# K and Q convolutions in a lane of their own, scaled outputs in the head's key and query tile, the learned tokens' masks in a stream of their own

## The chip, the core and the metric

The kernel runs on one core of a Trainium2 chip. Its engines are PE (TensorE, matrix products; PEld is its weight load), DVE (VectorE), ACT (ScalarE), POOL (GpSimd) and SP (SyncE, which here issues every DMA). Each engine works through its own list of instructions in a fixed order and stops at an instruction until what that instruction needs is there. The metric is the time of one execution on the device, in microseconds, as the median of several runs.

## What is computed

One layer of a bidirectional encoder: 1024 positions of width 1024, with 16 learned ("meta") tokens in front. The input projection gives queries, keys and values of 8 heads (128 wide), gates and two further branches. The part that the change touches is the gated delta rule, in chunks, forwards and backwards:

```python
qkv = silu(depthwise_conv_centred(concat([q, k, v]), conv_w))      # 5 taps
qc, kc = l2norm(q_heads) * DN_DK ** -0.5, l2norm(k_heads)
beta = sigmoid(b_raw);  g = -exp(A_log) * softplus(a_raw + dt_bias)
# chunk_gated_delta_rule, once forwards and once on the flipped sequence:
g = cumsum(g)
decay = exp(where(tri, g[:, None] - g[None, :], -inf))
lmat = where(strict, beta[:, None] * (k @ k.T) * decay, 0)
sol = triangular_solve(lmat + eye, [v * beta, k * beta * exp(g)])   # u, w
qk = (q @ k.T) * decay
for each chunk:                       # a scan with the state S
    v_new = u - w @ S
    o = (q * exp(g)) @ S + qk @ v_new
    S = S * exp(g_last) + (k * exp(g_last - g)).T @ v_new
o = o_fwd + o_bwd
o = o * rsqrt(mean(o * o) + eps) * norm_w * silu(z)
```

Behind it stand the projection of this output, a short convolution branch, the merge of both by sigmoid gates, an output projection and a SwiGLU feed-forward block. Everything is float32.

## The kernel before

Matrix products of float32 are made of three products of the fast fp32r type: each operand is split into a high part (an ACT cast) and the rest (a DVE subtraction). The delta rule itself uses plain float32 products.

The first half of the program (up to about 985 us) is one long interleaving. Its ground is the **dense** work: column blocks of 128 of the input projection, in the function `dense_steps` (line 332 of the profile), each of 24 products for a stretch of 320 to 512 positions. A block is called a unit: K, Q and V of each head (`u_qkv`), the z gates, the short branch (`u_short`), and as many merge gates as are not left for later. Into it go the **streams** of the delta rule, Python generators of which each runs for one head at a time: `g_decay` (decay masks into the tile PQ: one DMA, DVE additions, ACT exponentials), `g_norm` (transposes of keys and queries to token order; ACT copies the keys and squares both with 17 `Square` instructions, line 545, the token part; then the products k k^T and q k^T, line 583, from which DVE makes the tile NP, line 613), `g_inv` (the triangular inverse: 32x32 blocks by a DVE recurrence, lines 491 and 495, then products at lines 706 to 737 with ACT and DVE copies between them, T at line 708 among them) and `g_scan` (8 steps, forwards and backwards at once, lines 796 to 871, then normalization, scaling, transposes and the store of the output).

The order is found while the program is built. The planner keeps a clock for each engine (`T`), to which every instruction adds an assumed cost. After each three dense products `run_streams` lets every stream step that is due go on, and `pump` gives DVE convolution work while its clock is less than 0.7 us ahead of PE's. That work waits in **lanes**, of which `pump` takes the one with the least weighted time spent; the lane "short" gives way to all others. All convolutions of K, Q and V are in one lane, "conv", first come, first served. One convolution (`conv_job`) is, for each half of the positions, four DVE multiply-adds (line 355), an ACT tanh into a half buffer `rb` (line 360) and a DVE product (line 363). A new row buffer `ra` can be had only when the third job before it is done; if it is not, `force` issues what is left of it at once, whatever the planner's clocks say.

Buffers tie the heads together. The tile `kq` (keys and queries of a head, transposed) has 3 buffers, so K of head h takes that of head h-3 (`u_qkv`, `while freed < h - 2`, where `freed` counts heads whose last scan step has read its keys and queries). NP has 2 buffers: the scan adds up its outputs in the place of products that it has used (`oacc`), and the scaled, transposed and gated output `oT` goes into NP as well, from where it is stored to `o_d`. So NP of head h waits for that store of head h-2:

```python
while done < h - 1 or "PQ" not in st_:
    yield T["pe"] + 100
if h > 1:
    yield heads[h - 2]["stored"]
```

`done` counts finished scans and `stored` is the planner's time of the end plus 4 us. At the end of the scan, for each half: four ACT scalings in place (line 893), four PE transposes, one DVE product into NP (line 899), one store of 256 KB.

The masks of the learned tokens (`Dm`, 16x16 for each head) are made at the end of the stream `g_gates`: a DMA, a wait of 6 us in the planner's time, a DVE addition, eight ACT exponentials. `g_gates` stands in the same list as `g_decay`, so the first head's decay masks come behind it.

Of the kernel before, what the change touches and what calls it, by code (L numbers as in the profile page):

```python
# [16 lines left out]
P = 128  # L17
# [20 lines left out]
def encoder_layer(ctx: ExitStack, tc: tile.TileContext, x, meta, norm1_w, w_in,  # L38
# [208 lines left out]
    lanes = {"conv": [], "short": [], "fs": [], "norm": []}  # L247
    spent = {"conv": 0.0, "short": 0.0, "fs": 0.0, "norm": 0.0}
# [17 lines left out]
    WEIGHT = {"conv": 1.0, "short": 1.0, "fs": 0.33, "norm": 0.1}  # L266
# [34 lines left out]
    def pump():  # L301
        while T["dve"] <= T["pe"] + 700:
            now = max(T["dve"], T["pe"])
            cand = [k for k, q in lanes.items() if q and q[0].ready <= now + 20 + DEP * (k == "fs")]
            if "norm" in cand:
                cand = ["norm"]
            if not cand and any(q and q[0].ready <= now + DEP + 20 for q in lanes.values()):
                T["dve"] = now + DEP
                continue
            if not cand:  # L310
                if not rest or T["dve"] > T["pe"] + 100:
                    return
# [54 lines left out]
    def u_qkv(h, i, w):  # L367
# [163 lines left out]
    def g_norm(h, st_):  # L531
# [34 lines left out]
        nc.vector.tensor_tensor(out=Nm, in0=pt[:META, P:P + META], in1=Dm[:, h], op=ALU.mult)  # L566
# [27 lines left out]
        nc.vector.tensor_scalar(out=Nm, in0=Nm, scalar1=cc[:META, 8, 0:1], scalar2=None, op0=ALU.mult)  # L594
# [150 lines left out]
    def g_scan(h, st_):  # L745
# [142 lines left out]
        yield T["dve"] + 2300  # L888
        for c4 in range(2):
            oT = NP[:, 4 * c4:4 * c4 + 4, 1 - c4]  # L890
            pt = newbank()
            for c in range(4):
                nc.scalar.activation(oacc[4 * c4 + c], oacc[4 * c4 + c], AF.Copy, scale=y[:, 4 * c4 + c:4 * c4 + c + 1])
# [23 lines left out]
    decs, norms, invs, scans = [], [], [], []  # L917
# [28 lines left out]
    def start_streams():  # L946
# [9 lines left out]
        h = ninv  # L956
        if h < H and not invs and heads[h].get("normed"):
# [9 lines left out]
    def run_streams():  # L967
        nonlocal done
        again = True
        while again:  # L970
            again = False
            for q in (scans, invs, norms, decs):
                if q and q[0][1] <= T["pe"]:
                    again = True
                    r = next(q[0][0], None)
                    if r is None:
# [4 lines left out]
                        elif q is not decs:  # L981
# [220 lines left out]
    def g_gates():  # L1202
# [84 lines left out]

        nc.sync.dma_start(Dm, grow[:, 8, 0:1, 0:META].rearrange("h o i -> o h i").broadcast_to([META, 8, META]))
        yield T["pe"] + 6000
        nc.vector.tensor_tensor(out=Dm, in0=Dm, in1=mask2[:META, 0, :META].unsqueeze(1).broadcast_to([META, 8, META]), op=ALU.add)  # L1290
        yield small_v()
        for h in range(H):
            nc.scalar.activation(Dm[:, h], Dm[:, h], AF.Exp, bias=negG2[:META, 8, h:h + 1])
            A(16)
            if h % 2:
                yield T["act"]

    dn = ph1.enter_context(tc.tile_pool(name="dn", bufs=1))
# [632 lines left out]
```

## Time and profile before

| what | value |
|---|---|
| median of 3 runs | 1962.57 us (1962.05 to 1963.68) |
| the profiled execution's own time | 1961.08 us |
| its span, first to last instruction | 1959.4 us |
| granted TensorE clock, mean | 0.999 |
| PE busy | 1941.7 us, 99% of the span |
| DVE busy | 1468.1 us, 75% |
| ACT busy | 867.9 us, 44% |
| POOL busy | 158.4 us, 8% |

Busy times of PE are modelled from the starts of pipelined products, so one product's duration (some 340 ns) overlaps the next one's. In a list of groups the first number behind the bar is the busy time in us, the second the mean of one instruction in ns, the third the idle time of the engine just before these instructions. In a list of waits stand the total in us, how many there were, and the longest. "<-" in front of an engine names what ended a wait. In a timeline the columns are start, duration, engine, line, operation, tiles, shapes and count, and idle time before in brackets.

### The profile page before, as it was taken

Reading aid. Unit: us, or ns where it says so; the run is one execution under the profiler, and the core shown is the slowest. Engines: PE = TensorE matmul, PEld = TensorE weight load, DVE = VectorE, ACT = ScalarE, POOL = GpSimd, SP = SyncE. Lnnn points to the kernel's source line nnn. Section 1 sums busy time; section 2 is a strip of 40 time slices with the busy share of each in tenths; the row PEclk is TensorE's granted clock in tenths of the full one; section 3 lists DMA queues with packets and bytes.
Section 4 is the critical chain, followed back from the end, with each engine's and each line's share of the span. In section 5 each row is a group of like instructions: output and inputs, shape, how many; then the busy total and the mean of one; then the engine's idle time right before and its main releaser. Section 6 shows DMA issues by size and latency. Waiting matters only on the chain.

```text
span 1959.4 us, 31938 instructions
## 1 busy us (share of the span) xinstructions
PE 1941.7 (99%) x11962; PEld 1704.4 (87%) x11962; DVE 1468.1 (75%) x2804; ACT 867.9 (44%) x2014; POOL 158.4 (8%) x457
## 2 busy tenths in 40 slices
PE   8999999999999999999999999999999999999998
PEld 8998899999899999998888888887888888888887
DVE  4778778788887888787358798559787887756574
ACT  5463544646455554533445545234232332324343
POOL 3012112020110202110000000000000000000001
PEclk9999999999999999999999999999999999999999
DMA  4222332323222222224386623332666644587654
GB/s 146 68 76 80 103 99 60 87 60 87 60 76 67 85 65 79 70 69 153 103 310 246 206 88 121 115 119 73 212 232 209 209 165 163 179 279 243 194 181 155
DMA packets 243136, 264.11 MB, mean 135 GB/s; under 512 B 46820, under 2 KB 166933, under 8 KB 240549
## 3 DMA queue, kind: packets, MB, share of 16 engines
q1 hardware_dynamic: 242981, 262.07, 42.1%
q8 instruction: 94, 1.54, 0.3%
q14 instruction: 61, 0.50, 0.1%
HBM read 189.58 MB, written 72.44 MB: 134 GB/s over the span
## 4 chain that ended last, share of the span: by engine, by line
PE 89%; DVE 5%; ACT 3%; issue 1%; DMA 1%; POOL 0%; SPq 0%; POOLq 0%; DVEq 0%; ACTq 0%
PE pm L332 31%; PE pm L1382 5%; PE pd L1382 4%; PE pe L1382 3%; PE pm L1656 3%; PE pm L1658 3%; PE pm L1657 2%; PE pd L1658 2%; PE pd L1656 2%; PE pd L1657 2%; PE pe L1658 2%; PE pe L1656 2%; PE pe L1657 2%; PE pm L1814 1%; PE pm L1815 1%; PE pm L1813 1%
## 5 line engine op out<-in xcount | busy, mean ns | idle before, releaser
L332 PE MATMUL pm<-hTh,wh 128*128 128x512 f32 (+4 forms) x1328 | 483.8, 365 | 0.1
L332 PE MATMUL pm<-hTh,wl 128*128 128x512 f32 (+4 forms) x1328 | 450.5, 340 | 0.0
L332 PE MATMUL pm<-al,wh 128*128 128x512 f32 (+4 forms) x1328 | 449.6, 339 | 0.5 <-DVE al L1047 0.5
L332 PEld LDWEIGHTS pm<-hTh,wl 128*128 128x128 f32 x1328 | 249.1, 188 | 15.5
L332 PEld LDWEIGHTS pm<-hTh,wh 128*128 128x128 f32 x1328 | 250.2, 189 | 13.6 <-ACT hTh L1041 0.2
L332 PEld LDWEIGHTS pm<-al,wh 128*128 128x128 f32 x1328 | 250.4, 189 | 12.9 <-DVE al L1047 0.7
L87 DVE TENSOR_TENSOR al<-raw,ring_h 128x1024 fp32r<-128x1024 f32 x73 | 88.4, 1223 | 63.6 <-ACT ring_h L86 63.2
L86 ACT CAST ring_h<-raw 128x1024 fp32r<-128x1024 f32 x73 | 76.9, 1054 | 109.7 <-PE pd L1815 35.3
L940 DVE TENSOR_TENSOR wl<-raw,wh 128x512 fp32r<-128x512 f32 x122 | 84.1, 690 | 32.0 <-ACT wh L943 27.1
L355 DVE SCALAR_TENSOR_TENSOR kq<-ra,wc,kq 128x520 f32<-128x520 f32 (+1 forms) x128 | 95.9, 749 | 2.3 <-ACT kq L389 1.2
L821 ACT ACTIVATE w<-pd,small 128x128 f32<-128x128 f32 x128 | 40.2, 365 | 124.9 <-PE pd L814 106.4
L128 POOL TENSOR_SCALAR ss<-ss 128x1 f32<-128x1 f32 x13 | 4.6, 353 | 951.1 <-ACT b L1825 603.4
L491 DVE TENSOR_TENSOR tm<-fP,fN 128x135 f32<-128x135 f32 (+23 forms) x248 | 72.1, 291 | 10.0 <-DMA fN<-nd 3.3
L495 DVE TENSOR_TENSOR fP<-fP,tm 128x135 f32<-128x135 f32 (+23 forms) x248 | 71.8, 289 | 7.3
L943 ACT CAST wh<-raw 128x512 fp32r<-128x512 f32 x122 | 74.8, 619 | 0.1
L87 DVE TENSOR_TENSOR raw<-pair,raw 128x1024 fp32r<-128x1024 f32 (+1 forms) x42 | 48.0, 1143 | 30.4 <-ACT raw L86 30.4
L86 ACT CAST raw<-pair 128x1024 fp32r<-128x1024 f32 (+1 forms) x42 | 41.7, 992 | 58.4 <-PE pd L1382 27.5
L87 DVE TENSOR_TENSOR wl<-pair,wh 128x1024 fp32r<-128x1024 f32 (+1 forms) x42 | 48.1, 1144 | 21.7 <-ACT wh L86 21.6
L86 ACT CAST wh<-pair 128x1024 fp32r<-128x1024 f32 (+1 forms) x42 | 41.7, 992 | 46.0 <-PE pd L1382 24.7
L843 DVE SCALAR_TENSOR_TENSOR S<-S,eGl,pd 128x128 f32<-128x128 f32 x104 | 31.8, 344 | 38.2 <-PE pd L831 30.8
L130 POOL TENSOR_TENSOR small<-small,minus_half 128x9 f32<-128x9 f32 x16 | 29.5, 1842 | 353.8 <-DVE small L878 264.0
L661 POOL TENSOR_TENSOR tm<-mP,mN 1x15 f32<-1x15 f32 (+7 forms) x120 | 37.3, 311 | 237.0 <-DMA mN<-ndm 228.7
(660 smaller groups left out, 4945.7 us busy)
## 6 DMA issues: line engine op xcount, KB each, us to landing
raw<-in_w_in_dram SPq DMA_DIRECT2D x64, 512.0 KB
raw<-in_w_gate_up_dram SPq DMA_DIRECT2D x44, 512.0 KB
sums<-in_w_down_dram SPq DMA_DIRECT2D x22, 512.0 KB
t_d<-sums SPq DMA_DIRECT2D x11, 1024.0 KB
raw<-s_d SPq DMA_DIRECT2D x44, 256.0 KB
raw<-t_d SPq DMA_DIRECT2D x44, 256.0 KB
act_d<-b SPq DMA_DIRECT2D x43, 256.0 KB
raw<-act_d SPq DMA_DIRECT2D x33, 256.0 KB
```

What stands on the lines that cost most here:

```text
L86: nc.scalar.copy(hi, src)
L87: nc.vector.tensor_tensor(out=lo, in0=src, in1=hi.bitcast(F32), op=ALU.subtract)
L332: mm(po[:, :n], (wl if j == 2 else wh)[:, k], xl[k][:, t0:t0 + n] if j == 1 else xh[k][:, t0:t0 + n], start=(i == 0), stop=(i == 3 * KT - 1))
L355: nc.vector.scalar_tensor_tensor(out=acc, in0=raw[:, h0 + t:h0 + t + hn], scalar=wc[:, t, col:col + 1], in1=acc, op0=ALU.mult, op1=ALU.add)
L491: nc.vector.tensor_tensor(out=tv, in0=fP[:, 0:r, j:j + 1].broadcast_to([P, r, n]), in1=fN[:, j:j + 1, j + 1:32].broadcast_to([P, r, n]), o ...
L495: nc.vector.tensor_tensor(out=fP[:, 0:r, j + 1:32], in0=fP[:, 0:r, j + 1:32], in1=tv, op=ALU.subtract)
L940: nc.vector.tensor_tensor(out=u[1][1][:, k], in0=u[2][:, k], in1=u[1][0][:, k].bitcast(F32), op=ALU.subtract)
L943: nc.scalar.copy(u[1][0][:, k], u[2][:, k])
L1382: mm(bank[t], a[:, c], b, start=fresh, stop=first and k == 3 and j == 2, skip_group_check=not first)
L1656: mm(po, ah[:, k], bhk, start=k == 0, stop=False)
L1657: mm(po, ah[:, k], blk, start=False, stop=False)
L1658: mm(po, al[:, k], bhk, start=False, stop=k == 3)
```

## The change

Five things are altered.

1. **Lanes.** K and Q convolutions go to a new lane "kq" whose time counts a fifth; "conv" holds V alone, and gives way whenever another lane can go on.
2. **Scaled outputs.** At the end of a scan the eight scaled outputs go to the key half of the head's own `kq` tile (`osc`), no longer in place into NP, and all eight are scaled before the first transpose. The gated output `oT` goes to the query half of `kq` and is stored from there. NP of head h then waits for the scaling of head h-2 ("scaled"), and no longer for its store.
3. **K's buffer.** Since `kq` is now in use up to the store, K of head h waits for `done` and no longer for `freed`.
4. **The masks.** The end of `g_gates` becomes a stream `g_meta` in a list of its own, which starts once the first `g_decay` has; its exponentials end with `gated`.
5. **Nm.** The learned tokens' product is copied from PSUM as it is (before: multiplied by `Dm` there); the multiplication by `Dm` is done later, together with that by beta, after `gated`.

```diff
-    lanes = {"conv": [], "short": [], "fs": [], "norm": []}
+    lanes = {"kq": [], "conv": [], "short": [], "fs": [], "norm": []}
-    WEIGHT = {"conv": 1.0, "short": 1.0, "fs": 0.33, "norm": 0.1}
+    WEIGHT = {"kq": 0.2, "conv": 1.0, "short": 1.0, "fs": 0.33, "norm": 0.1}
             if len(cand) > 1 and "short" in cand:
                 cand.remove("short")
+            if len(cand) > 1 and "conv" in cand:
+                cand.remove("conv")
@@ u_qkv
-                    while freed < h - 2:
+                    while done < h - 2:
-                job = enqueue("conv", conv_job(raw, dst, col, sub, META if i == 1 else 0))
+                job = enqueue("conv" if i == 2 else "kq", conv_job(raw, dst, col, sub, META if i == 1 else 0))
@@ g_norm
-        nc.vector.tensor_tensor(out=Nm, in0=pt[:META, P:P + META], in1=Dm[:, h], op=ALU.mult)
+        nc.vector.tensor_copy(Nm, pt[:META, P:P + META])
...
-        nc.vector.tensor_scalar(out=Nm, in0=Nm, scalar1=cc[:META, 8, 0:1], scalar2=None, op0=ALU.mult)
+        while not gated:
+            yield T["pe"] + 100
+        nc.vector.scalar_tensor_tensor(out=Nm, in0=Nm, scalar=cc[:META, 8, 0:1], in1=Dm[:, h], op0=ALU.mult, op1=ALU.mult)
         on("dve", 950)
-        while done < h - 1 or "PQ" not in st_:
+        while "PQ" not in st_ or h > 1 and "scaled" not in heads[h - 2]:
             yield T["pe"] + 100
         if h > 1:
-            yield heads[h - 2]["stored"]
+            yield heads[h - 2]["scaled"]
@@ g_scan
+        osc, oTs = (kq[:, a, 0:SEQ].rearrange("p (c t) -> p c t", c=NC) for a in range(2))
+        t = [0, 0]
+        for c in range(NC):
+            nc.scalar.activation(osc[:, c], oacc[c], AF.Copy, scale=y[:, c:c + 1])
+            t[c // 4] = A(P)
+        st_["scaled"] = t[1]
         for c4 in range(2):
-            oT = NP[:, 4 * c4:4 * c4 + 4, 1 - c4]
+            oT = oTs[:, 4 * c4:4 * c4 + 4]
             pt = newbank()
+            yield t[c4]
             for c in range(4):
-                nc.scalar.activation(oacc[4 * c4 + c], oacc[4 * c4 + c], AF.Copy, scale=y[:, 4 * c4 + c:4 * c4 + c + 1])
-                t = A(P)
-            yield t
-            for c in range(4):
-                transpose(pt[:, c], oacc[4 * c4 + c])
+                transpose(pt[:, c], osc[:, 4 * c4 + c])
@@ the driver: a fifth list of streams, metas, started by start_streams
+        if ndec == 1 and not metas and not gated:
+            metas.append([g_meta(), T["dve"] + HOP, None])
-            for q in (scans, invs, norms, decs):
+            for q in (scans, invs, norms, decs, metas):
@@ g_gates ends here
+    def g_meta():
         nc.sync.dma_start(Dm, grow[:, 8, 0:1, 0:META].rearrange("h o i -> o h i").broadcast_to([META, 8, META]))
         yield T["pe"] + 6000
         nc.vector.tensor_tensor(out=Dm, in0=Dm, in1=mask2[:META, 0, :META].unsqueeze(1).broadcast_to([META, 8, META]), op=ALU.add)
-        yield small_v()
+        yield on("dve", 240)
...
+        gated.append(True)
```

Since the planner sets the order from its clocks, instructions move on every engine. The number of PE products is the same in both programs, 10352. Three places follow, all on ACT. In these rows a line number of the changed kernel is that of its own file (360 became 362, 389 became 391, 545 became 547, 708 became 712, 821 became 825, 893 became 896, 943 became 950).

First place, an inversion: the forced rest of a V convolution. `rb<-vT` is the tanh of V's convolution, `wh<-raw` the cast of a weight block, `ra` and `kq` are the copies of a dense stretch of K or Q out of its PSUM bank, and `T<-pd` is the copy for which the inverse's next product on PE waits. Before, in the inversion of head 3:

```order
L360 ACTIVATE rb_6171<-vT_4642 128x520
L388 COPY ra_6174<-pm_6123 128x322
L389 ACTIVATE kq_5962<-pm_6123,wc 128x322
L943 CAST wh_6119<-raw_5896 128x512
L708 ACTIVATE T_992_6183<-pd_6184 128x256
```

In the changed kernel, in the inversion of head 2:

```order
L362 ACTIVATE rb_4886<-vT_3594 128x520
L390 COPY ra_4889<-pm_4845 128x322
L391 ACTIVATE kq_4729<-pm_4845,wc 128x322
L950 CAST wh_4841<-raw_4657 128x512
L712 ACTIVATE T_762_4901<-pd_4902 128x256
```

The same five instructions stand in the same order, one head earlier; in head 3's inversion the nearest tanh of V now stands 13 rows ahead of T.

Second place, the scan of head 2, two of its steps: `w` and `v` are the copies that PE's next products of the scan need, `jk` the squares. Before:

```order
L821 ACTIVATE w_5604<-pd_5562,small_2619 128x128
L821 ACTIVATE w_5606<-pd_5562,small_2619 128x128
L826 ACTIVATE v_881_5608<-pd_5562,small_2619 128x128
L826 ACTIVATE v_882_5610<-pd_5562,small_2619 128x128
L388 COPY ra_5520<-pm_5525 128x320
L389 ACTIVATE vT_4642<-pm_5525,wc 128x320
L871 ACTIVATE jk_5640,small_2619<-NP_3502 128x128
L871 ACTIVATE jk_5644,small_2619<-NP_3502 128x128
L821 ACTIVATE w_5687<-pd_5652,small_2619 128x128
L821 ACTIVATE w_5689<-pd_5652,small_2619 128x128
```

In the changed kernel (`small_2511` is head 2's, `small_5504` head 4's):

```order
L875 ACTIVATE jk_5654,small_2511<-NP_3407 128x128
L390 COPY ra_5575<-pm_5580 128x320
L391 ACTIVATE vT_4730<-pm_5580,wc 128x320
L576 COPY kn_5506<-pe_5608 128x256
L547 ACTIVATE jk_5681,small_5504<-pe_5608 128x128
L547 ACTIVATE jk_5683,small_5504<-pe_5608 128x128
L547 ACTIVATE jk_5685,small_5504<-pe_5608 128x128
L547 ACTIVATE jk_5687,small_5504<-pe_5608 128x128
L825 ACTIVATE w_5709<-pd_5665,small_2511 128x128
L825 ACTIVATE w_5711<-pd_5665,small_2511 128x128
```

The key copies and squares of head 4 have moved between the steps of head 2's scan. By the order before, only head 2's squares stand inside a scan (head 0's); in the changed one those of heads 4, 5, 6 and 7 do (in the scans of heads 2, 3, 4 and 5), and head 2's do not.

Third place, the end of head 2's scan and the first copies of K of head 5, which takes head 2's `kq` buffer. Before:

```order
L893 ACTIVATE NP_3502<-NP_3502,small_2619 128x128 x4
L943 CAST wh_5894<-raw_5708 128x512
L360 ACTIVATE rb_5941<-kq_4641 128x520
L388 COPY ra_5964<-pm_5898 128x336
L389 ACTIVATE kq_5962<-pm_5898,wc 128x336
L943 CAST wh_5894<-raw_5708 128x512
L764 ACTIVATE vS_5956<-pd_5957,small_4625 128x128 x3
```

In the changed kernel:

```order
L896 ACTIVATE kq_1348<-NP_3407,small_2511 128x128 x8
L950 CAST wh_5969<-raw_5764 128x512 x2
L362 ACTIVATE rb_6032<-vT_4730 128x520
L390 COPY ra_6045<-pm_5973 128x336
L391 ACTIVATE kq_6043<-pm_5973,wc 128x336
L768 ACTIVATE vS_6057<-pd_6058,small_4432 128x128 x3
L768 ACTIVATE vS_6057<-pd_6068,small_4432 128x128 x3
```

The rows are close to what they were, but `kq_6043` now takes the buffer of `kq_1348`, which four rows above has just been written and from which the output is still to be made and stored.

More of the change, by code (lines that the diff above doesn't have):

```diff
@@ L245, in step @@
             return T["dve"] - max(t0, T["pe"])
-    lanes = {"conv": [], "short": [], "fs": [], "norm": []}
-    spent = {"conv": 0.0, "short": 0.0, "fs": 0.0, "norm": 0.0}
+    lanes = {"kq": [], "conv": [], "short": [], "fs": [], "norm": []}
+    spent = {"kq": 0.0, "conv": 0.0, "short": 0.0, "fs": 0.0, "norm": 0.0}
     def enqueue(lane, gen):
@@ L916, in encoder_layer @@
     done = freed = near = 0
-    decs, norms, invs, scans = [], [], [], []
+    decs, norms, invs, scans, metas = [], [], [], [], []
     def qkv_ok():
@@ L980, in run_streams @@
                             heads[h]["stored"] = T["pe"] + STORE
-                        elif q is not decs:
+                        elif q is not decs and q is not metas:
                             heads[h]["inverted" if q is invs else "normed"] = True
@@ L1296, in g_gates @@
                 yield T["act"]
+        gated.append(True)
+    gated = []
     dn = ph1.enter_context(tc.tile_pool(name="dn", bufs=1))
```

## The prediction

> **What bounds the kernel now.** I read first the busy times and the chain of work that ended last, then busy time by stretch, then PE's own waits.
>
> ```profile
> span 1959.4 us, 31938 instructions
> PE 1941.7 (99%) x11962; PEld 1704.4 (87%) x11962; DVE 1468.1 (75%) x2804; ACT 867.9 (44%) x2014; POOL 158.4 (8%) x457
> PE 89%; DVE 5%; ACT 3%; issue 1%; DMA 1%; POOL 0%; SPq 0%; POOLq 0%; DVEq 0%; ACTq 0%
> ```
>
> PE is busy for 99% of the span, and 89% of the chain runs through it. The edits add and remove no product (10352 in either program). So a gain can only come out of what PE waits, and a loss only out of new waits. Where are they? By stretch (bounds, length, then busy time of PE, PEld, DVE, ACT, POOL, then clock, DMA share, GB/s):
>
> ```profile
> 0.00:42.00 42.00, 36.87 (x257) 33.34 (x257) 22.58 (x38) 24.86 (x51) 17.73 (x42) 1.00 0.56 170
> 42.00:985.00 943.00, 939.14 (x7388) 871.49 (x7389) 733.02 (x1872) 473.61 (x1497) 125.03 (x382) 1.00 0.29 81
> 985.00:1225.00 240.00, 240.00 (x1059) 198.49 (x1058) 191.35 (x208) 120.50 (x149) 0.00 (x0) 1.00 0.58 197
> 1318.00:1742.00 424.00, 422.31 (x1872) 348.80 (x1871) 344.40 (x481) 136.30 (x173) 1.08 (x2) 1.00 0.55 184
> ```
>
> All edits lie in the second row, the interleaved part after the start. There PE idles 943.00 - 939.14 = 3.9 us in all. The next stretch has no idle time: the delta rule ends while dense units are left, so a scan that ends earlier shortens nothing. Who made PE wait in the second row:
>
> ```profile
> PE pd L714 <- ACT T L708: 1.7, 1, 1.7
> PE pd L796 <- DVE S L843: 0.6, 1, 0.6
> PE pd L814 <- DVE r L806: 0.5, 2, 0.3
> PE pd L729 <- POOL small L130: 0.4, 1, 0.4
> PE pd L730 <- POOL fP L643: 0.2, 1, 0.2
> ```
>
> That is 3.4 of the 3.9 us, in six waits. Some loss hides inside pipelined products, where no idle time shows:
>
> ```profile
> L834 PE MATMUL pd<-v,PQ 128*128 128x128 f32 x256 | 39.0, 275 | 0.0
> L831 PE MATMUL pd<-w,kn 128*128 128x128 f32 x224 | 35.8, 282 | 0.0
> ```
>
> Equal shapes, 7 ns apart in the mean: 224 x 7 ns = 1.6 us, from products whose `w` came a little late. With it the most that any order can win here is 3.9 + 1.6 = 5.5 us. A loss has no such bound.
>
> **The change part by part.** The sum starts from the profiled execution, 1961.08 us (its span of 1959.4 and 1.7 around it); the median of the three runs, 1962.57, is 1.5 above it.
>
> *Lanes.* The longest wait, 1.7 us at L714, has this history on ACT and DVE:
>
> ```profile
> 487.68 0.61 ACT L943 CAST wh<-raw 128x512 fp32r<-128x512 f32 x1
> 489.53 1.55 DVE L355 SCALAR_TENSOR_TENSOR vT<-ra,wc,vT 128x520 f32<-128x520 f32 x2
> 491.12 0.64 ACT L360 ACTIVATE rb<-vT 128x520 f32<-128x520 f32 x1 [2.83 <-DVE vT L355]
> 491.66 0.41 ACT L388 COPY ra<-pm 128x322 f32<-128x322 f32 x1
> 492.90 0.40 ACT L708 ACTIVATE T<-pd 128x256 f32<-128x256 f32 x1
> 495.50 0.42 ACT L388 COPY ra<-pm 128x320 f32<-128x320 f32 x1
> ```
>
> A V convolution is forced out at a stroke: two multiply-adds on DVE, and the tanh that needs them. ACT stands 2.83 us in front of the tanh, and the copy T, four rows behind it, is late for PE. The change should make this rarer for K and Q, but it makes V wait longer in its lane, so V's rest is what gets forced. The order shows the very same five rows in head 2's inversion, and not in head 3's. So I book -1.7 and +1.7: nothing. The bounds are -1.7 (the multiply-adds happen to be done earlier in the new place) and +1.7 (a second such place; V's tanh also stands between copies of head 5's inversion).
>
> *Scaled outputs, and what they let start.* ACT does the same eight scalings, DVE the same two products, SP the same two stores in each scan:
>
> ```profile
> L893 ACT ACTIVATE NP<-NP,small 128x128 f32<-128x128 f32 x64 | 19.9, 390 | 11.1 <-POOL small L130 11.1
> L899 DVE SCALAR_TENSOR_TENSOR NP<-pd,cols,vS 128x512 f32<-128x512 f32 x16 | 11.9, 746 | 7.2 <-PE pd L83 7.1
> L545 ACT ACTIVATE jk<-pe 128x128 f32<-128x128 f32 (+1 forms) x136 | 38.3, 281 | 3.1
> L545 ACT ACTIVATION_READ_ACCUMULATOR jk<-pe 128x1 f32 (+1 forms) x136 | 27.1, 199 | 0.0
> ```
>
> The first store leaves about four scalings later (4 x 0.39 = 1.6 us at most); nothing reads `o_d` in this stretch, so that costs nothing; if the store were late, K's buffer below would be late with it. What counts is that norms now run earlier: the 17 squares of a head (0.28 + 0.20 us each) stand between the steps of a scan for four heads, before for one. What is behind them on ACT are `w` and `v`, for which PE's L831 and L834 wait, and then S on DVE. The one case in the trace is head 2's squares in head 0's scan:
>
> ```profile
> 229.63 0.62 ACT L821 ACTIVATE w<-pd,small 128x128 f32<-128x128 f32 x2
> 230.28 0.22 DVE L491 TENSOR_TENSOR tm<-fP,fN 128x31 f32<-128x31 f32 x1 [3.30 <-DMA fN<-nd]
> 233.40 0.36 ACT L861 ACTIVATE NP<-pd,eG 128x128 f32<-128x128 f32 x1
> 234.03 0.59 DVE L843 SCALAR_TENSOR_TENSOR S<-S,eGl,pd 128x128 f32<-128x128 f32 x2
> 236.66 0.60 DVE L806 SCALAR_TENSOR_TENSOR r<-pd,negEG,vS 128x128 f32<-128x128 f32 x2
> ```
>
> PE waited 0.6 us for this S and 0.3 for this r, 0.9 in the scan. But `w` was in time, and DVE was late for a reason of its own: it had stood 3.30 us for the recurrence's input, a DMA. So an overlapped head costs between 0 and 0.9 us; I take 0.3, nearer the lower end, since the squares themselves are not what the row blames. Three heads more: +0.9, bounds 0 and 2.7. Where squares and norm leave, something is saved: the waits at L729 and L730 (0.4 + 0.2) fall where head 6's norm meets head 5's inverse; the products of the norm still meet an inversion, so I take -0.6 with bounds -0.6 and 0.
>
> *K's buffer.* K of head h+3 must now wait for the store of head h, with ACT as the one that waits. It is tight for head 5 alone, where two casts, a tanh and a copy (2 x 0.61 + 0.64 + 0.41 = 2.3 us) stand between. In the same time PE transposes, DVE multiplies (0.75), and the store lands. No view shows a store of the output landing; the nearest row is SP's wait for other stores, and for the transposes a group of four:
>
> ```profile
> SPq L676 <- DMA pd<-fP: 32.7, 8, 6.1
> ```
>
> ```profile
> 483.81 0.60 PE L83 MATMUL pe<-ident,kq 128*128 128x128 f32 x4
> ```
>
> A store is waited for 4.1 us in the mean and 6.1 at the longest. ACT then stands 0.6 + 0.75 + 4.1 - 2.3 = 3.2 us, up to 5.2; no less than 0. PE goes on into two more dense stretches with other PSUM banks; one takes 3.8 us (the copies at 491.66 and 495.50, a wait among it), so some 7 us hide it, and I book 0. With that cover gone, nine copies of V and the inversion's copies behind it would be late too, and it costs up to 5.2. The Trainium skill, "DMA: Bandwidth & Descriptors", section "Anatomy of one DMA — SWDGE (gpsimd) path", puts a fixed 2.0 us on each DMA, most of it the receipt of the write, plus bytes over 436 GB/s: by it, as an estimate, 2.6 us for 256 KB and a stand of 1.7 us. By that rule this wait could be struck out as a rival; the row's 4.1, with other stores and loads in flight, speaks for keeping it.
>
> *Masks and Nm.* Eight 16x16 products from PSUM become copies and eight scalings get a third operand:
>
> ```profile
> L566 DVE TENSOR_TENSOR Nm<-pe,Dm 16x16 f32<-16x16 f32 x8 | 1.3, 160 | 8.3 <-ACT jk L545 8.3
> L594 DVE TENSOR_SCALAR Nm<-Nm,small 16x16 f32<-16x16 f32 x8 | 1.8, 222 | 0.3
> ```
>
> 0.16 and 0.22 us each, hidden under PE, as is the earlier start of head 0's decay (a few us, with only dense work depending on PE then). Nothing; were a whole one more of them in PE's path for each head, it would be 8 x 0.22 = 1.8 us.
>
> Sum: 1961.08 + 0 + 0.9 - 0.6 + 0 + 0 = 1961.4 us as a profiled execution, and with the 1.5 us to the median **1962.9 us**. Own range: -1.7 - 0.6 below and +1.7 + 2.7 above, 1960.3 to 1967.0.
>
> **The rivals.** A measurement of this kernel tells about 0.2%, 3.9 us, from no change; so faster begins below 1958.7 and slower above 1966.5.
>
> *The waits go (faster).* The new hand-off frees NP and the lanes end the bursts, so that all idle time and the hidden 1.6 go: 1962.57 - 5.5 = 1957.1 us. For it: each wait has a neighbour that is moved. Against it: 4.5 us or more of 5.5 would have to go, and the largest wait's rows stand there again.
>
> *The squares delay the scans (slower).* If PE itself waits out a group of four squares (4 x 0.48 = 1.9 us) once in each of the four overlapped scans, that is 7.7 us, less the 0.9 that head 0's scan loses now: 1962.57 + 6.8 = 1969.4. It decides from about 0.6 of a group per scan on. For it: four groups stand ahead of `w` in each of these scans. Against: in the one case `w` came in time, and the planner's clocks count these squares.
>
> *ACT stands for K's store.* If the 7 us of cover are taken by scan work, 5.2 us reach PE, once: 1967.8. Against: head 5 alone is tight.
>
> That the change does not do what it says, since scans were not held up by NP's store, changes no time and lies within the forecast.
>
> **How the numbers follow.** Forecast 0.62, the waits go 0.13, squares 0.18, K's store 0.07. Of the forecast nearly all is within 0.2%, a little (0.02) above. Faster: 0.13 less a little that stays above the bound, 0.12. Slower: 0.18 less 0.03, half of 0.07, and 0.02, 0.21; the rest, 0.67, is the same. The range takes in most of the first rival and the better half of the squares: 1958.0 to 1968.5.
>
> **What would show it.** Right: PE busy near 939 of 943 us between 42 and 985; a wait of 1 to 2 us for T in head 2's inversion, none in head 3's; ACT waiting for a DMA before K of head 5, with no PE wait behind it; PE still full when the last scan ends, and that earlier than before. Wrong: idle time of over 4 us before L796, L814 or L831 (in the changed kernel's numbers a few lines further), with squares just ahead on ACT; or a PE wait for a bank of K.

## The result and the profile after

Five runs of the changed kernel have a median of 1981.37 us (1979.34 to 1982.33), five of the kernel before 1962.32 us (1961.89 to 1963.68). The ratio is 1.0097, with an interval of 1.0085 to 1.0108: the change costs 19 us, and the time lies 12.9 us above the predicted range.

All of it lies where the prediction looked, in the interleaved part between 42 and 1000 us. The first rows are the head of the page and that stretch of the changed kernel, the next the same stretch of the kernel before (bounds, length, busy time of PE, PEld, DVE, ACT, POOL, clock, DMA share, GB/s).

```profile
span 1979.5 us, 31949 instructions
PE 1949.0 (98%) x11962; PEld 1709.2 (86%) x11962; DVE 1466.3 (74%) x2804; ACT 867.0 (44%) x2014; POOL 165.3 (8%) x457
42.00:1000.00 958.00, 940.80 (x7368) 871.71 (x7369) 731.26 (x1872) 472.51 (x1497) 132.08 (x383) 0.99 0.28 79
1000.00:1240.00 240.00, 240.00 (x1059) 198.31 (x1058) 186.77 (x202) 119.22 (x148) 0.00 (x0) 1.00 0.56 195
```

```profile
42.00:1000.00 958.00, 954.14 (x7454) 883.91 (x7455) 738.50 (x1879) 477.59 (x1504) 125.03 (x382) 1.00 0.30 84
```

PE idles 958.00 - 940.80 = 17.2 us instead of 3.9, so 13.3 us more. The rest of the loss is in the products themselves: in the whole program PE is busy for 1949.0 - 1941.7 = 7.3 us more, with the same 11962 products. The column before the last two shows why: the granted clock is 0.99 instead of 1.00. PE's own waits in the changed kernel, and the one wait on ACT that the kernel before does not have:

```profile
PE pe L585 <- DVE PQ L621: 10.9, 8, 4.7
PE pe L83 <- ACT jk L547: 4.3, 2, 3.6
PE pd L800 <- DVE S L847: 1.9, 1, 1.9
ACT kq L391 <- DMA o_d<-kq: 6.0, 2, 5.1
```

The longest wait, at head 5, read from PE back to its origin. Rows of the timeline (start, length, engine, line, operation, count, and in brackets the idle time before it with what ended it):

```profile
478.39 0.42 ACT L390 COPY ra<-pm 128x336 f32<-128x336 f32 x1
478.84 1.58 SPq L909 DMA_DIRECT2D o_d<-kq  x2
483.92 0.54 ACT L391 ACTIVATE kq<-pm,wc 128x336 f32<-128x336 f32 x1 [5.11 <-DMA o_d<-kq]
484.35 2.42 ACT L768 ACTIVATE vS<-pd,small 128x128 f32<-128x128 f32 x9
486.60 0.75 ACT L529 ACTIVATE PQ<-PQ,negG 128x128 f32<-128x128 f32 x2
487.10 0.64 DVE L617 SCALAR_TENSOR_TENSOR NP<-pe,small,PQ 128x128 f32<-128x128 f32 x2 [2.81 <-ACT PQ L529]
489.38 0.42 DVE L621 TENSOR_TENSOR PQ<-pe,PQ 128x256 f32<-128x256 f32 x1
489.95 1.19 PE L585 MATMUL pe<-kq 128*128 128x256 f32 x2 [4.71 <-DVE PQ L621]
491.26 0.52 PE L334 MATMUL pm<-al,wh 128*128 128x384 f32 x1
```

ACT reaches the first copy of K of head 5 at 478.8 and stands 5.11 us until the second store of head 2's output has landed, because that store reads the very buffer. Behind this copy stand, in ACT's order, nine copies `vS` and then the exponentials `PQ` (L529) of head 4; DVE's product into `NP` (L617) waits for these, DVE's `PQ` (L621) comes behind it (with a step of K's convolution between them, which stood 0.97 us for K's second copy on ACT), and only that one gives back the bank `pe` that PE's next products of keys and queries (L585) need. PE had dense work until 485.2, 6.4 us after the first store was issued, and stood then for 4.71 us.

The last row shows a second loss. A dense product of 384 columns takes 0.52 us behind the wait; ahead of it such a product took 0.34:

```profile
484.90 0.34 PE L334 MATMUL pm<-hTh,wl 128*128 128x384 f32 x1
```

The clock by stretches shows this around the three longest waits:

```profile
484.00:487.50 3.50, 1.24 (x8) 0.92 (x6) 0.69 (x3) 3.50 (x13) 0.90 (x5) 1.00 0.73 132
487.50:494.33 6.83, 4.38 (x13) 4.23 (x14) 5.73 (x13) 3.59 (x10) 0.00 (x0) 0.50 0.13 40
494.33:500.00 5.67, 5.67 (x97) 5.38 (x96) 4.85 (x11) 3.55 (x10) 0.42 (x2) 1.00 0.01 4
647.90:651.30 3.40, 3.40 (x15) 3.11 (x14) 1.93 (x7) 1.22 (x8) 0.00 (x0) 0.50 0.01 2
699.10:702.50 3.40, 3.40 (x13) 3.40 (x12) 3.24 (x9) 1.09 (x3) 0.00 (x0) 0.50 0.00 0
```

Half clock in three places, 6.83 + 3.41 + 3.41 = 13.65 us; in the profile of before this stretch has none. PE worked for 4.38 + 3.40 + 3.40 = 11.2 of these microseconds (the first place still holds 2.45 us of the wait), and at half clock such work costs half of its time, 5.6 us. Over the whole program PE idles 12.8 us more (1979.5 - 1949.0 against 1959.4 - 1941.7), which with the 7.3 us of longer products makes the 20.1 by which the spans differ. Of the 7.3 the clock explains 5.6; the other 1.7 are not assigned here.

ACT stands at K's first copy for two more heads, 6 and 7:

```profile
586.74 0.54 ACT L391 ACTIVATE kq<-pm,wc 128x336 f32<-128x336 f32 x1 [0.90 <-DMA o_d<-kq]
693.80 0.54 ACT L391 ACTIVATE kq<-pm,wc 128x336 f32<-128x336 f32 x1 [3.31 <-issue]
```

PE waits there for 1.29 and 2.85 us. The trace names no releaser for the second one; the queue of SP does, as far as it goes. It issued the second store of head 4's output late, since transfers of the inverse's recurrence (`pd<-fP`, `pdm<-mP`) stood ahead of it, and sent a weight block of 512 KB right behind it:

```profile
683.33 0.32 SPq L909 DMA_DIRECT2D o_d<-kq  x1
683.70 1.68 SPq L675 DMA_DIRECT2D pd<-fP  x3
686.00 0.33 SPq L909 DMA_DIRECT2D o_d<-kq  x1
686.41 1.56 SPq L940 DMA_DIRECT2D raw<-in_w_in_dram  x1
```

So K's buffer accounts for up to 4.7 + 1.3 + 2.85 = 8.9 us of PE's waits and, behind the first and the last, for (4.38 + 3.40) / 2 = 3.9 us of clock: some 13 of 20. The other large wait, 3.62 us at 643.9 in head 4's scan, is of another kind:

```profile
640.53 1.54 DVE L413 SCALAR_TENSOR_TENSOR rb<-ra,cols,rb 128x512 f32<-128x512 f32 x2
642.50 1.54 DVE L413 SCALAR_TENSOR_TENSOR rb<-ra,cols,rb 128x512 f32<-128x512 f32 x2
644.56 0.59 DVE L847 SCALAR_TENSOR_TENSOR S<-S,eGl,pd 128x128 f32<-128x128 f32 x2
645.39 0.37 ACT L865 ACTIVATE NP<-pd,eG 128x128 f32<-128x128 f32 x1 [4.25 <-DVE NP L871]
647.54 0.80 PE L83 MATMUL pe<-ident,kq 128*128 128x128 f32 x4 [3.62 <-ACT jk L547]
```

Here a short convolution was forced at a stroke on DVE ahead of the scan's state `S` and of the addition into `NP` (L871), and ACT stood 4.25 us in front of its own `NP` (L865). Behind that stand, on ACT, a key copy and four squares of head 6's norm (645.90 to 647.49), and only they give back the bank for PE's next transposes. So the squares that have moved into the scan take part in this wait, with 1.6 us. With its 3.41 us of half clock it comes to 3.6 + 1.7 = 5.3 us.

### The profile page after: what moved, and what is told of

Read it like the earlier page. It is cut to its first block, busy times and chain, and to the rows that moved or that the text cites. A ratio compares the mean times of both kernels' runs of the same rounds, so it can differ in the third digit from the quotient of the medians.

```text
span 1979.5 us, 31949 instructions
## 1 busy us (share of the span) xinstructions
PE 1949.0 (98%) x11962; PEld 1709.2 (86%) x11962; DVE 1466.3 (74%) x2804; ACT 867.0 (44%) x2014; POOL 165.3 (8%) x457
## 4 chain that ended last, share of the span: by engine, by line
PE 90%; DVE 5%; ACT 2%; DMA 1%; issue 1%; SPq 0%; POOL 0%; POOLq 0%; ACTq 0%; DVEq 0%
PE pm L334 32%; PE pm L1395 5%; PE pd L1395 4%; PE pe L1395 3%; PE pm L1669 2%; PE pm L1671 2%; PE pm L1670 2%; PE pd L1669 2%; PE pd L1671 2%; PE pd L1670 2%; PE pe L1671 2%; PE pe L1669 2%; PE pe L1670 2%; PE pm L1827 1%; PE pm L1828 1%; PE pm L1826 1%
## 5 line engine op out<-in xcount | busy, mean ns | idle before, releaser
L334 PE MATMUL pm<-hTh,wh 128*128 128x512 f32 (+4 forms) x1328 | 487.5, 368 | 0.1
L334 PEld LDWEIGHTS pm<-al,wh 128*128 128x128 f32 x1328 | 251.9, 190 | 12.9 <-DVE al L1056 0.7
L390 ACT COPY ra<-pm 128x320 f32<-128x320 f32 (+3 forms) x72 | 32.3, 449 | 59.1 <-PE pm L334 58.8
```

The source lines that it names most:

```text
L334: mm(po[:, :n], (wl if j == 2 else wh)[:, k], xl[k][:, t0:t0 + n] if j == 1 else xh[k][:, t0:t0 + n], start=(i == 0), stop=(i == 3 * KT - 1))
```

## The experiments

Two theories stood after this. By theory A, ACT's stand in front of K's buffer, its tail of ACT and DVE work and the clock behind it make most of the loss. The rival: the many moved instructions do it, by lanes, squares and masks that crowd DVE and ACT, and the store is only the wait that comes last by the profile. Later a third was added, theory O: what is left without the buffer's wait is what any reordering of this program does. Below, "idle" is PE's idle time between 42 and 1000 us of the profiled execution.

### The changed kernel without the shared buffer

The scaled outputs go into the head's normed keys `kn`, for which the copies of K don't ask, and K has only its old condition.

```diff
-                    while done < h - 2:
+                    while freed < h - 2:
-        osc, oTs = (kq[:, a, 0:SEQ].rearrange("p (c t) -> p c t", c=NC) for a in range(2))
+        osc = oTs = kn[:, 0:NC]
```

> The changed kernel, with the scaled and the gated output in the head's token-order key tile kn (free once the scan is over, wanted again only by a norm three heads later) and K waiting for the last scan step again, so that K's first copy no longer waits for a store. The computation is the same. Theory A (ACT stands for the store before K's first copy; PE waits 4.7 + 1.3 + 2.8 us behind it, and the clock is halved for 6.8 + 3.4 us after the two long ones, which costs 5.1): these 14 us go, about 1967 us; no ACT wait for o_d; a long PE wait in head 4's scan (3.6 us, and 1.7 of clock) stays. Theory B (the earlier norms, with their squares inside the scans, cost the time): 1978 to 1983, since they stay where they are.

Measured: 1969.35 us (1966.44 to 1970.15), ratio to the kernel before 1.0034, interval 1.0021 to 1.0047. ACT no longer waits for a store there.

```profile
42.00:1000.00 958.00, 948.87 (x7422) 877.25 (x7422) 730.39 (x1872) 474.57 (x1501) 132.12 (x384) 1.00 0.28 80
PE pe L585 <- DVE PQ L621: 4.4, 8, 1.3
PE pd L800 <- DVE S L847: 2.5, 1, 2.5
PE pd L818 <- DVE r L810: 1.1, 3, 0.6
```

12.0 of the 19 us are gone. That bears theory A out, and it speaks against the rival: the squares of heads 4 to 7 still stand in the scans of heads 2 to 5 here, and PE's waits there come to 1.1 us for the scans (the three for `r`) and 0.33 for a bank that squares give back. But it is no clean pair, since K's other condition moves instructions too. The 3.6 us wait in head 4's scan went as well, because `S` (at 633.22) now stands ahead of the forced burst (from 634.67) on DVE. In head 0's scan, on the other hand, the wait for `S` grew from 1.9 to 2.5 us and is now followed by 3.41 us at half clock. And waits of 0.74 and 1.29 us for the norm's bank stay where the changed kernel has 1.29 and 2.85, so not all of those two was the store's. 7.5 us stay.

### The scaled outputs alone, in the shared buffer and out of it

A cleaner pair: to the kernel before, only the scaled outputs and the earlier norm are added, without lanes and masks. In the first kernel the outputs go into `kq`, in the second into `kn`. Each engine's instructions stand in the same order in both; only the buffers differ.

```diff
-                    while freed < h - 2:
+                    while done < h - 2:
...
-        while done < h - 1 or "PQ" not in st_:
+        while "PQ" not in st_ or h > 1 and "scaled" not in heads[h - 2]:
...
-            yield heads[h - 2]["stored"]
+            yield heads[h - 2]["scaled"]
...
+        osc, oTs = (kq[:, a, 0:SEQ].rearrange("p (c t) -> p c t", c=NC) for a in range(2))
```

> The kernel before with the scaled outputs in kq, NP's wait for the scaling and K's wait for the whole scan alone: no lane of K and Q, masks as before. By the order, K of heads 5, 6 and 7 follows right behind the end of the scan whose buffer it takes. Theory A: each of these three stands 3 to 5 us on ACT and costs 3 to 5 us on PE, with half a clock behind those over some 2.5 us: 12 to 22 us slower than before, 1974 to 1984. Theory B (squares in scans): by the order no squares stand inside a scan but head 2's, as before, so within 3 us of before, 1960 to 1966.

The second one, against the first:

```diff
-                    while done < h - 2:
+                    while freed < h - 2:
-        osc, oTs = (kq[:, a, 0:SEQ].rearrange("p (c t) -> p c t", c=NC) for a in range(2))
+        osc = oTs = kn[:, 0:NC]
```

> The same as the kernel with the scaled outputs alone, and instruction for instruction in the same order, but with the outputs in kn instead of kq, so that K's copy has no store to wait for. Theory A: 1960 to 1967, all of the loss of its neighbour gone, no halved clock. Theory B: like its neighbour, whatever that gives.

Measured, in `kq`: 1985.87 us (1985.43 to 1986.03), ratio 1.0122, interval 1.0106 to 1.0139, a little more than expected, and head 4's K stood as well. In `kn`: 1960.17 us (1959.44 to 1960.83), ratio 0.9992, interval 0.9983 to 1.0001. First the rows in `kq` (the stretch, ACT's wait, PE's wait, and the clock around the first one), then those in `kn`:

```profile
42.00:1000.00 958.00, 936.63 (x7350) 869.81 (x7349) 734.04 (x1872) 472.16 (x1498) 124.07 (x383) 0.99 0.27 78
ACT kq L389 <- DMA o_d<-kq: 22.3, 4, 8.1
PE pe L83 <- DVE Nm L566: 18.1, 4, 6.8
379.90:381.80 1.90, 0.00 (x0) 0.00 (x0) 0.00 (x0) 0.88 (x2) 0.00 (x0) 1.00 0.71 113
381.80:388.60 6.80, 3.89 (x14) 3.89 (x15) 4.04 (x8) 6.04 (x26) 0.00 (x0) 0.50 0.20 50
```

```profile
42.00:1000.00 958.00, 955.01 (x7459) 884.18 (x7460) 742.07 (x1880) 475.68 (x1504) 123.24 (x383) 1.00 0.29 84
PE pd L796 <- DVE S L843: 1.0, 1, 1.0
```

The wait for the store is worth 1985.87 - 1960.17 = 25.7 us by itself: 958.00 - 936.63 = 21.4 against 3.0 us of idle time, and 23.9 us at half clock (four places) against none. ACT stands for four heads here, 5.6 us in the mean. With order and work the same on every engine, the buffer alone decides over this time: theory A is shown. About the squares this pair says nothing. In both kernels they stand where they stood before, only head 2's inside a scan (head 0's, at 222 to 237 us). So the scaled outputs are not what moves the norms into earlier scans.

### The lanes alone, and each other part with the outputs in `kn`

The lanes alone are the change's new lane, its weight, V's giving way and the line that fills the lane, and no more:

```diff
+            if len(cand) > 1 and "conv" in cand:
+                cand.remove("conv")
...
+                job = enqueue("conv" if i == 2 else "kq", conv_job(raw, dst, col, sub, META if i == 1 else 0))
```

> The kernel before with the lane for K and Q (and V's yielding) alone; outputs, buffers and masks as before. The changed kernel with the outputs in a tile of their own was still 7.5 us slower than before, while the scaled outputs in that tile alone were not slower; so the rest belongs to lanes or masks, or to what both do to the order. Theory L (V's convolutions, forced at a stroke, delay products and copies): 1965 to 1970, with named PE waits behind forced V work. Theory M (the masks): within 3 us of before, 1959 to 1965.

Lanes and scaled outputs together, the outputs in `kn`:

> Lanes and the scaled outputs in kn; masks as before. Theory L: 1965 to 1970, no wait for o_d on ACT. Theory M: 1958 to 1964.

Masks in a stream of their own and scaled outputs together, the outputs in `kn`, without the lanes:

```diff
-        nc.vector.tensor_tensor(out=Nm, in0=pt[:META, P:P + META], in1=Dm[:, h], op=ALU.mult)
+        nc.vector.tensor_copy(Nm, pt[:META, P:P + META])
...
+    def g_meta():
```

> The masks' stream and the later product with them, and the scaled outputs in kn; one lane for all convolutions, as before. Theory L: 1958 to 1964. Theory M: 1965 to 1970, most of it from the wait in head 0's scan (DVE late with S because it stood for the inversion's input), 2 to 3 us and 1.7 of clock.

Measured: lanes 1965.94 us (1965.35 to 1967.34), ratio 1.0021, interval 1.0011 to 1.0030; lanes and outputs 1969.95 (1968.07 to 1971.10), 1.0042, 1.0027 to 1.0056; masks and outputs 1968.21 (1966.77 to 1968.55), 1.0031, 1.0019 to 1.0042. Idle times 7.4, 9.2 and 6.7 us. The waits are small and scattered, the longest in each of the three kernels 1.6, 1.5 and 1.6 us; for lanes alone, and for masks and outputs:

```profile
PE pe L83 <- ACT jk L547: 2.4, 2, 1.6
PE pe L585 <- DVE PQ L619: 2.0, 3, 0.9
```

```profile
PE pe L583 <- DVE PQ L619: 3.2, 3, 1.6
```

Each time lies in the range of one theory, but not by the waits that the theory named: the one of 2 to 3 us in head 0's scan, expected with the masks, did not come. In the kernel with the lanes alone the squares of heads 4 to 7 do stand in the scans of heads 2 to 5, as in the changed kernel; so it is the lanes that move them, and PE's waits there are 0.64 us for `r`, 0.25 for `v` and 0.77 for a bank behind squares. The parts don't add up either: outputs in `kn` -1.6 us, lanes +3.9, both +7.9 and not +2.3. Is it the parts, or the order?

### A number that means nothing

The planner's constants `DEP` and `HOP` (the assumed waits in ns of DVE for its own last result, and of one engine for another's) set its clocks and so the order of the work, but no work. Two of them are changed a little in the kernel before, and one in the kernel with the outputs in `kn`.

```diff
-    HOP, TOPE, DEP = 200, 370, 127
+    HOP, TOPE, DEP = 200, 370, 132
```

> The kernel before with one number of the planner changed, which has no meaning for the computation: the assumed wait of DVE for its own last result 132 ns instead of 127. The instructions are the same, their order is another one. Theory O (any other order than the one before loses some microseconds, since the one before has waits of 3.9 us only where a usual order has 7 to 9): 1964 to 1970, with PE's idle time between 42 and 1000 us at 6 to 9 us. Theory P (lanes and masks themselves cost what they cost in the last runs): within 2 us of before, 1960 to 1964.

```diff
-    HOP, TOPE, DEP = 200, 370, 127
+    HOP, TOPE, DEP = 210, 370, 127
```

> The same with another number, the assumed way of a result from PE to another engine, 210 ns instead of 200. By the order the last dense blocks run out before the last scan ends, which adds about 1 us to either. Theory O: 1965 to 1971. Theory P: 1961 to 1965.

The first of the two edits, on top of the scaled outputs in `kn`:

> The scaled outputs in a tile of their own (1960.2 us before) with the assumed wait of DVE at 132 ns. Theory O: 1963 to 1970. Theory P: 1959 to 1962.

Measured, with ten runs each against 25 of the kernel before:

| edit | us | ratio (interval) | idle, us |
|---|---|---|---|
| `DEP` 132 in the kernel before | 1960.33 | 0.9992 (0.9983 to 1.0002) | 2.4 |
| `HOP` 210 in the kernel before | 1966.22 | 1.0022 (1.0012 to 1.0031) | 8.0 |
| `DEP` 132 with outputs in `kn` | 1966.30 | 1.0024 (1.0014 to 1.0033) | 7.5 |

The stretches of the second and the third:

```profile
42.00:1000.00 958.00, 950.01 (x7431) 880.28 (x7432) 733.25 (x1873) 477.35 (x1501) 125.16 (x383) 1.00 0.29 81
```

```profile
42.00:1000.00 958.00, 950.50 (x7433) 879.30 (x7434) 734.04 (x1874) 476.29 (x1502) 124.55 (x382) 1.00 0.28 82
```

Two of three meaningless edits cost 4.3 and 6.1 us against the kernel that they start from, as much as lanes (3.9) or masks (1968.21 - 1960.17 = 8.0, somewhat more than either) do; the third costs nothing, and with its 2.4 us of idle time it contradicts the part of theory O that any other order loses. So the 4 to 8 us that stay without the buffer's wait are of the size of a reordering. That the lanes or masks cost something of their own beyond this is neither shown nor excluded; it would take many orders of each.

### The clock behind a wait

Two kernels put a small chain of products and copies into the kernel before, so that PE waits for ACT for a set time. The extra results are used for nothing. In the first, the chain stands in the last feed-forward loop:

```diff
+        if j in PROBE:
+            pz = psany()
+            transpose(pz[:, 0:P], ident)
+            nc.scalar.copy(probe, pz[:, 0:64])
+            for _ in range(PROBE[j]):
+                nc.scalar.copy(probe, probe)
+            transpose(pz[:64, P:2 * P], probe)
```

> The kernel before with five waits of PE put into the feed-forward stretch (where it has none), some 60 us apart: a transpose, a chain of 6, 10, 13, 16 and 21 small dependent ACT copies (64 columns), a transpose of the result. PE should stand about 1.6, 2.4, 3.0, 3.6 and 4.6 us. If a wait is followed by half a clock from some length between 1.9 us (which in the changed kernel was not) and 2.85 us (which was) on, the first two cost their own length alone, and the last three their length and 1.7 to 3.4 us more each; the granted clock after each shows it. In all 15 us of waits, and 5 to 10 of clock: 1982 to 1988.

Measured in one profiled execution: 1973.34 us. It largely missed its aim, since other products filled four of the five gaps. The one that stayed, a wait of 3.97 us at 1410.3, was followed by 6.83 us at half clock:

```profile
PE pe L83 <- ACT probe L1776: 4.5, 2, 4.0
1412.20:1419.00 6.80, 4.77 (x12) 3.81 (x13) 2.35 (x4) 1.59 (x6) 0.00 (x0) 0.50 0.89 280
```

In the second the same chain stands six times between two halves of the merge gate's blocks, where the order is written by hand:

```diff
+    PROBE = {1: 4, 2: 6, 3: 8, 4: 10, 5: 12, 6: 15}
...
+            if i and j in PROBE:
```

> The kernel before with six waits of PE put into the dense work, each between the two halves of a merge-gate block, the first about 840 and the last about 975 us from the start: a transpose, a chain of 5, 7, 9, 11, 13 and 16 small ACT copies (0.24 us each in the earlier probe), a transpose of the result. PE should stand about 1.4, 1.9, 2.4, 2.8, 3.3 and 4.0 us, 15.8 in all, if ACT has nothing else to do. If half a clock follows from some 2.5 us on: three times 3.4 to 6.8 us at half, 5 to 10 us of loss, 1983 to 1988. If the halving is a matter of how the wait falls into fixed stretches of time, some waits of 1.4 to 2.4 us have it too, and some longer ones not: 1981 to 1990. If it takes more than 3.4 us, one of six: 1979 to 1981.

Measured in one profiled execution: 1996.57 us, 34.5 more than the 1962.04 of the kernel before on the same chip.

```profile
PE pm L83 <- ACT probe L459: 21.4, 6, 5.2
906.00:914.00 8.00, 6.21 (x34) 5.03 (x33) 4.54 (x7) 3.00 (x11) 0.00 (x0) 1.00 0.56 207
928.32:931.73 3.41, 3.12 (x10) 2.73 (x11) 0.69 (x1) 1.28 (x5) 0.00 (x0) 0.50 0.40 160
948.80:955.60 6.80, 5.93 (x19) 5.06 (x20) 1.74 (x7) 1.65 (x6) 0.00 (x0) 0.50 0.01 3
```

The six waits took 1.79, 2.34, 3.27, 5.22, 4.00 and 4.82 us. Behind the first the clock stayed full; behind the others it was at half for 3.41, 6.83, 6.83, 6.83 and 3.41 us. Of these 27.3 us PE worked for 23.3 (in the others the wait was still going on), and that work costs half of its time, 11.7 us. With 21.4 us of waits this makes 33.1. A sixth stretch of 3.41 us, behind the wait at the inverse's L714 that the kernel before has too, adds 1.7: 34.8 us, where the spans differ by 1994.9 - 1959.4 = 35.5. So a wait of PE costs its length and, if it is long enough, here 1.6 to 3.0 us on top.

## Why the prediction was wrong

**The step that failed is "some 7 us hide it, and I book 0", in the part on K's buffer.** It measured some 13 us of a sum of 20, and 25.7 us where the scaled outputs were added alone. The mechanism was named rightly, down to the store, the waiting engine, head 5 and the copies of V behind it, but three things in its price failed.

- *The cover was the wrong one.* The 7 us were dense stretches with other PSUM banks. PE did have 6.4 us of dense work. But PE's next order was not for a bank of K; it was for a bank of the norm, whose release runs through ACT's exponentials and DVE behind the stand. That chain of 6 us (483.92 to 489.95) filled the dense work by itself. ACT stood 5.11 us and PE waited 4.71: the free cover was 0.4 us.
- *It is not tight for head 5 alone.* PE waited at heads 6 and 7 as well; without the lanes ACT stood for heads 4 to 7. The prediction looked at rows between store and copy in one place of the order and gave the others away without a number.
- *The clock was in no term.* "It costs up to 5.2" was the length of a stand, and 5.11 was measured. But a long wait of PE is followed by half clock, which cost 3.9 us in these places; in the stretch that the change alters, the profile of before has none by which this could be seen. With up to 3.0 us of it a single stand of 5.2 us costs some 8, and there were three stands.

The store's time itself was well bounded: the 4.1 us in the mean, 6.1 at most, that other stores took, against 5.1 from the issue of head 2's first output store to the end of the stand (478.84 to 483.92). The estimate from the Trainium skill, "DMA: Bandwidth & Descriptors", a stand of 1.7 us, was too low by a factor of three in this place; its section is on DMAs that GpSimd issues, and SP issues these. Had the rival been struck out by that rule, as that sentence considered, the only case with the right mechanism would have been lost. It stood at a chance of 0.07 and 1967.8 us.

**Lanes: 0, with bounds of 1.7.** The forced tanh of V did move to head 2's inversion. There ACT stood 3.10 us (2.83 before), but PE did not wait for T. It waited 0.74 us for the bank of a norm, which DVE's `PQ` gave back behind the same forced work on V:

```profile
396.34 0.64 ACT L362 ACTIVATE rb<-vT 128x520 f32<-128x520 f32 x1 [3.10 <-DVE vT L357]
398.12 0.39 ACT L712 ACTIVATE T<-pd 128x256 f32<-128x256 f32 x1
398.19 0.67 PE L585 MATMUL pe<-kq 128*128 128x256 f32 x2 [0.74 <-DVE PQ L621]
```

So the wait of 1.7 us went and a smaller one came; at these places the term held within its bounds, though not by the wait that it named. But the lanes alone measured +3.9 us, outside their bounds, in small waits for the norm's squares and `PQ` that the term did not have; a meaningless reordering makes as many. The burst of the short convolution in head 4's scan, 5.3 us with its clock, was not seen either. It counts as a miss of the sum, though not as shown to be the lanes' doing.

**Squares +0.9, saved waits -0.6.** The size is borne out, the cause is not. With the squares inside four scans and the outputs in `kn`, PE's waits in these scans were 1.1 us and 0.33 for a bank, near 0.3 for each head, and the waits at L729 and L730 did go. But the prediction put the moved norms down to the scaled outputs, and they come with the lanes: the scaled outputs alone, in `kn`, left the squares in their places and measured -1.6 us (interval -3.3 to +0.2). The rival that PE waits out four squares, 1969.4 at 0.18, happened once in place of four times, in head 4's scan: 1.6 of the 3.6 us there, for a bank of the norm and not for `w`. Its time is near that of three kernels here, which do not have such waits for `w`.

**Masks and Nm 0.** Neither shown nor refuted: with the outputs in `kn` the masks add 8.0 us, of the size of a reordering (6.1).

**"No more than 5.5 us can be won; a loss has no such bound".** Both hold. (By its own bound 3.9 of the 5.5 us, not 4.5, would have had to go for a faster kernel; and the traces count 11962 products in either kernel, not 10352, which changes nothing in the argument.) The best kernels, at 1960.17 and 1960.33, win about 1.6 us, and neither is clearly faster. What the sum lacked is a term for the second half of that sentence: a program of which PE is busy for 99% of the span by a planner's order has its small waits placed by that order, and any move deals them anew. Two of three such moves cost 4 to 6 us, and the third nothing.

**What would show it.** PE full after the last scan: right (240.00 of 240.00). That the scan ends earlier: wrong, the products of its last step end at 967.4 us instead of 962.2. ACT waiting for a DMA before K of head 5: right; "with no PE wait behind it": wrong. The sign announced for an error, a PE wait for a bank of K, would have missed this one, since the bank waited for was the norm's.

The 1.5 us between the profiled execution and the median of before may have their reason in the clock too, which is argued and not shown. Among the 25 executions of before beside the reorderings the spans follow the granted clock: 1958.8 us in the mean at 1.000 (2 of them), 1959.9 at 0.999 (13), 1961.0 at 0.998 (10). The profile of before, 1959.4 us at 0.999, has no half clock behind its wait of 1.7 us at L714; in the two kernels with chains, which contain the same wait, it was followed by 3.41 us at half clock. That fits the grid of the last section, by which it depends on where the wait falls.

## What to carry to other kernels

When a buffer's release is moved onto a store, take the engine that will stand in front of it and write down everything behind it in its order, up to the next thing that PE needs; cover is what is left beside that chain, not the dense work that PE has in hand. Price each PE wait of over about 2 us with what the half clock behind it costs, here 1.6 to 3.0 us. And where an order is planned, time a few meaningless reorderings before a few microseconds are put down to an edit.

## What the runs showed of the hardware

The half-clock times lie on a grid. In the changed kernel they begin at 487.5, 647.9 and 699.1 us, 47.0 and 62.0 times 3.413 us after the first; in the kernel with six chains at 494.83, 928.32, 948.80, 972.70, 993.18 and 1013.66, whole multiples of 3.413 apart as well (127, 6, 7, 6 and 6). Each lasts one or two steps of the grid, and begins at a step's end. What counts is idle time inside one step: waits that left about 2 us or more in one step were followed by half clock in all kernels here (1.91 at the least), while 1.79 us was not, nor 1.90 us in the changed kernel's head 0, of which 1.6 fell into one step. The plainest case is the kernel with `HOP` 210: a wait of 2.36 us at 504.2, split into 0.65 and 1.71 by the grid, kept the full clock, and one of 2.44 us at 709.4, with 2.14 in one step, did not. After the first step at half a second one followed where 0.83 us or more of the wait ran on into the first, and none where it was 0.5 us or less. The wait at L714 is the exception in length, 1.67 us among products of 32x32, but not in kind: in the two kernels with chains all of it lies in one step, and half clock follows; in the profile of before the grid, carried back from the half-clock stretch at its end (1956.94 us), splits it into 0.95 and 0.73, and none does.

The Trainium skill, "TensorE: Matmul & The Clock Gate", section "What's actually happening", has a free-running window of 3413 ns, which these traces agree with. Its section "HAM oscillation — how this bites in real kernels" puts the limit at idle gaps of over some 3.4 us; here 2.34 us among dense products were enough, and 1.91 where they fell into one step, and the measurement decides.

A store whose own instruction is short can still be late as a release: ACT stood up to 8.1 us for one of 256 KB, where other transfers were in flight.
